# The norm of the SSD branch, the turned softmax statistics and the order of the first loads in a hybrid decoder layer

## The chip, the cores and the metric

The kernel runs on one core of one Trainium2 chip. The core has a matmul engine (PE, whose weight loads are listed apart as PEld), a vector engine (DVE), a scalar engine (ACT), a general engine (POOL), and the queue of SyncE (SP), which issues most of the DMAs; ACT issues a few. Each engine works through its own instructions in order and waits on semaphores for the others. The metric is the device time of one execution in microseconds (us), here as the median of three runs.

## What is computed

One layer of a decoder on x of shape (1, 512, 1024) in float32: norm, one projection of 1024 x 10,128, three branches side by side (dilated window attention, causal pooling, a Mamba-2 state-space branch, called SSD here), gates, an output projection, and a feed-forward block with a convolution. These are the parts that matter here:

```python
def rmsnorm(x, g):
    xf = x.astype(jnp.float32)
    y = xf * lax.rsqrt(jnp.mean(xf * xf, axis=-1, keepdims=True) + NORM_EPS)
    return (y * g.astype(jnp.float32)).astype(x.dtype)
...
    m = jnp.max(scores, axis=-1, keepdims=True)
    p = jnp.exp(scores - m)
    l = jnp.sum(p, axis=-1)
...
    lse = m[..., 0] + jnp.log(l)
...
    y = y.reshape(b, s, SSD_INNER) * jax.nn.silu(z.astype(jnp.float32))
    yg = y.reshape(b, s, SSD_GROUPS, SSD_INNER // SSD_GROUPS)
    yg = yg * lax.rsqrt(jnp.mean(yg * yg, axis=-1, keepdims=True) + NORM_EPS)
    y = yg.reshape(b, s, SSD_INNER) * norm_w.astype(jnp.float32)
```

The attention is done in three groups of six heads; each gives an output, a maximum and a sum per head and position, and the three groups are combined by a softmax over m + log(l). The SSD branch has two groups of 512 channels, each normed over its channels.

## The kernel before

**Number format.** A large product is made of three matmuls in the type fp32r (a rounded float32): each operand is split into a high part (a cast on ACT) and a low part (the difference, on DVE), and high x high, high x low and low x high are added in PSUM (`mm3`, L228). Small products are plain float32, and PE executes each of those as two passes, so that a count of matmuls in the trace is twice that in the code.

**Jobs and steps.** The large products are a list of jobs (`program`, L1430). A job loads its weights through SP into one of two buffers (`fetch`, L174), ACT casts the high part in two halves (`cast`, L186), DVE makes the low part (`low`, L219), and PE multiplies. At the start of job n the low part of job n+1, the casts of n+2 and the load of n+3 are written out. After each chunk of 128 output channels (24 matmuls of 128 x 512) the kernel calls `step` (L156), which advances every small task that is under way (attention items, SSD items, norms) by one `yield`. A `yield WHOLE` puts the part that follows behind the others' parts of the same step. The order of the instructions on PE, ACT, DVE and POOL is the order in which the code writes them out; only SP's order is left to the scheduler.

**Start.** x is loaded as four blocks of 128 rows in two halves each (`load_x`, L1498): block 0 by SP, block 1 by ACT, then ACT loads the identity matrix `eye` (L1506) and the gain of the first norm, and SP the first two weights and blocks 2 and 3. PE multiplies `ones` with itself twelve times meanwhile (L1515). The squares of a half row are summed on ACT or DVE (`squares`, L433); the factor of a block goes into a diagonal matrix (`diag`, L1586, made from `eye`), and PE turns and scales x in one matmul with it (L1574). For block 1 both halves are squared on ACT (L1579). `turned` (L1541, instructions L1544 and L1545) writes the high and low part of the result, and `begin` (L1548, matmuls L1557) starts the first two jobs on it. Blocks 2 and 3 are scaled on ACT and DVE (L1609, L1611) and turned by PE at L1622.

**Attention statistics.** In each group, `nm` holds the negated maxima and `ls` the sums, 128 positions x 4 blocks x 6 heads. `stats` (L781) turns each by four PE transposes into a PSUM tile `pst`, and DVE copies the 6 x 512 result (L788). After the third group, `combine` (L796) works out the weights: minima, differences, exponentials on ACT, sums, a reciprocal on DVE (L811), three products on POOL (L815), a store to DRAM (`wd`), and loads of it spread over partitions (`wb`, L822), two for each of nine tiles. POOL multiplies the nine attention outputs by them (L824), three for each pair of heads.

**Norm of the SSD branch.** z is multiplied onto y on DVE (L1088) and squared on ACT (L1090); the squares of a group's four tiles (128 channels x 512 positions each) are added by POOL, and the last one by DVE (L1094). `y_norm` (L1096) then does this for each group: four float32 matmuls with the tile of squares as the stationary operand and one column of ones (L1104) give the sums per position in a column form, `rstd_of` (L418) makes the factor of 4 columns with a square root on ACT and one Newton step on DVE, DVE spreads the factors into four diagonal blocks `dg` (L1108), three steps later a matmul of `ones` with `dg` (L1115) puts them into all rows of a PSUM tile `prb`, and DVE multiplies y by the norm weight and by `prb` (L1118). High and low parts follow (L1120, L1125), for `w_c`.

**Order around the norms.** `MIX` (L1674) is "ZZ0zz1ggggaa": two jobs for z of group 0, the norm of group 0 queued, two jobs for z of group 1, the norm of group 1 queued, four jobs of the third gate, two jobs of the attention branch; then the SSD branch's output product, which needs both norms. `combine` runs in the same steps.

Of the kernel before, what the change touches and what calls it, by code (L numbers as in the profile page):

```python
# [10 lines left out]
F32 = mybir.dt.float32  # L11
# [5 lines left out]
P = 128  # L17
S = 512
# [65 lines left out]
def trunk(ctx: ExitStack, tc, out, x, rel_bias, ln1_g, w_in, b_gate, w_a, pool_w, pool_scale, w_b,  # L84
# [23 lines left out]
    def T(name, dt=F32, shape=(P, S)):  # L108
        return big.tile(list(shape), dt, name=name, tag="t")
# [4 lines left out]
    def SM(name):  # L114
        return psum.tile([P, S], F32, name=name, tag="sm")
# [3 lines left out]

    eye = cpool.tile([P, P], F32, name="eye")  # L120
    tri = cpool.tile([P, P], F32, name="tri")
    ones = cpool.tile([P, P], F32, name="ones")


    waiting, running = [], []
# [440 lines left out]
    def blocked(ap, g):  # L566
        return ap.rearrange("p (r j) -> p r j", r=4) if g == 0 else perm(ap, g)
# [2 lines left out]
        return ap if g == 0 else ap.rearrange("p (r j) -> p r j", r=4)  # L570

    dtr = cpool.tile([P, 4, SH], F32, name="dtr")
    V, QK, OT, NM, LS = {}, {}, {}, {}, {}

    def v_jobs(g):
# [129 lines left out]
                                                          lambda i, ps: emit("q", 1, i, r3[i], ps))]  # L705

    def attend(g):
        nm = cpool.tile([P, 4, HEADS], F32, name=f"nm{g}")
        ls = cpool.tile([P, 4, HEADS], F32, name=f"ls{g}")
        if g == 0:  # L710
            banks = [[(1, 0, 2), (2, 1, 2)], [(3, 2, 2), (0, 0, 1)]]
        else:
# [67 lines left out]

        def stats():  # L781
            yield WHOLE
            for src, store, nme in ((nm, NM, "nmT"), (ls, LS, "lsT")):
                ps = SM("pst")
                for n in range(4):
                    pe.transpose(ps[:HEADS, n * P:(n + 1) * P], src[:, n, :], eye)
                t = T(nme)
                dve.tensor_copy(blocked(t[:HEADS], g), grouped(ps[:HEADS], g))  # L788
                store[g] = t

        fill([item(2 * c + hh, nb, bank) for c in range(3) for nb, bank in enumerate(banks)
              for hh in range(2)] + [after(2, stats())])
# [111 lines left out]
    def ssd_prep():  # L904
# [36 lines left out]
        yield WHOLE  # L941
        ps = SM("pcs")
        pe.matmul(ps[:, :n16], tri, a, start=True, stop=True)
        pe.matmul(ps[:, n16:2 * n16], ones, a, start=True, stop=True)
        for i, r in enumerate((dr, gr)):
            pe.transpose(ps[:, 2 * n16 + 8 * i:2 * n16 + 8 * i + 8], r[:8, :P], eye[:8, :8])
        dve.tensor_copy(dgc, ps[:, 2 * n16:2 * n16 + 16])
        acs, tot, dec = (f(nme) for nme in ("acs", "tot", "dec"))
        dve.tensor_copy(acs, ps[:, :n16])
        dve.tensor_copy(tot, ps[:, n16:2 * n16])  # L950
        dve.tensor_tensor(dec, tot, acs, OP.subtract)
# [31 lines left out]

    def ssd_item(c, gi):
        cs = slice(c * P, (c + 1) * P)
        dtv, acs, dec, tot, ad, ed = (cst[n] for n in ("dtv", "acs", "dec", "tot", "ad", "ed"))
        als = []
        for q in range(2):
            al = T("al")
# [106 lines left out]
    def y_norm(gi):  # L1096
        while len(SQ[gi]) < 4:
            yield
        yield
        yield  # L1100
        yield WHOLE
        ps = SM("pss")
        for tb in range(4):
            pe.matmul(ps[:, tb:tb + 1], SQ[gi][0][:, tb * P:(tb + 1) * P], ones[:, :1],  # L1104
                      start=True, stop=True)
        r = rstd_of(ps[:, :4], 4, S)
        dg = T("dg")
        dve.tensor_tensor(dg.rearrange("p (b t) -> p b t", b=4), eye.unsqueeze(1).to_broadcast([P, 4, P]),  # L1108
                          r.unsqueeze(2).to_broadcast([P, 4, P]), OP.mult)
        yield  # L1110
        yield
        yield
        yield WHOLE
        ps = SM("prb")
        pe.matmul(ps, ones, dg, start=True, stop=True)  # L1115
        for j in range(4):
            y, m = Y[gi][:, j, :], 4 * gi + j
            dve.scalar_tensor_tensor(y, y, cst["dgc"][:, 8 + m:9 + m], ps, OP.mult, OP.mult)  # L1118
            yh, yl = T("yth", F32R), T("ytl", F32R)
            act.copy(yh, y)  # L1120
            YT[m] = (yh, yl)
            if j % 2:
                yield
                for q in (m - 1, m):
                    dve.tensor_sub(YT[q][1], Y[gi][:, q % 4, :], YT[q][0].bitcast(F32))  # L1125
# [369 lines left out]

    xin, warm = {}, small("warm", [P, 1])

    def load_x(tb, eng=sp):  # L1498
        for h in range(2):
            t = xin[tb, h] = T("xin")  # L1500
            eng.dma_start(t, x[tb * P:(tb + 1) * P, h * S:(h + 1) * S])

    g8, g1 = T("g8"), cpool.tile([P, KD], F32, name="g1")
    load_x(0)
    load_x(1, act)
    act.dma_start(eye, c_eye)  # L1506
    act.dma_start(g8[:KD, :P], ln1_g[0].rearrange("(k p) -> k p", p=P))
    dve.memset(ones, 1.0)
    dve.memset(warm, 1.0)
    act.activation(warm, warm, AF.Sqrt)  # L1510
    first = [MM("pa") for _ in range(4)]

    def warm_up(n):
        for i in range(n):
            pe.matmul(first[3][:, :P], ones, ones, start=True, stop=True)  # L1515

    fetch(weights[0], 2)
    fetch(weights[1])
# [57 lines left out]
    for tb in range(2):  # L1576
        s0, s1, v, sq, r, rt = (small(n, [P, 1]) for n in ("s0", "s1", "v", "sq", "r", "rt"))
        squares(act, xin[tb, 0], s0)
        squares((dve, act)[tb], xin[tb, 1], s1)  # L1579
        dve.tensor_scalar(v, s0, 1.0 / D, EPS, OP.mult, OP.add)  # L1580
        dve.scalar_tensor_tensor(v, s1, 1.0 / D, v, OP.mult, OP.add)
        act.activation(sq, v, AF.Sqrt)
        dve.reciprocal(r, sq)
        dve.scalar_tensor_tensor(rt, r, v, r, OP.mult, OP.mult)
        dve.tensor_scalar(rt, rt, -0.5, 1.5, OP.mult, OP.add)
        dve.tensor_scalar(diag[tb][:, :P], eye, r, rt, OP.mult, OP.mult)  # L1586
        if tb == 0:
            for k in range(KD):
                turn_scale(0, k)
# [116 lines left out]
```

## Time and profile before

| | us |
|---|---|
| median of three runs (1039.3 to 1040.51) | 1039.63 |
| the profiled execution | 1039.95 |
| its span, from the first to the last instruction | 1038.0 |
| PE busy in 0 to 14 | 11.00 of 14 |
| PE busy in 505 to 570 (both norms, `combine`) | 65.00 of 65 |
| DVE busy in 505 to 570 | 47.95 of 65 |
| ACT busy in 505 to 570 | 34.43 of 65 |
| PE busy in 692 to 990 (feed-forward block) | 297.96 of 298 |
| PE busy in 990 to 1038 | 40.82 of 48 |

Busy times are those of instructions that an engine executes; a matmul overlaps the next one, so the distance between starts tells more of PE than the length of one. A line of the timeline has start, length, engine, line, operation, output <- inputs, shapes and count, and in brackets the idle time before it and what ended that. A line of the windows has the window, its length, busy time and count for PE, PEld, DVE, ACT and POOL, then the granted clock of PE as a share of full speed, the busy share of the DMA engines, and GB/s. The queue of SP is called q1 in the DMA views, that of ACT q10.

### The profile page before, as it was taken

What the parts mean: (1) busy time and instruction counts of PE and PEld (TensorE: products, weight loads), DVE (VectorE), ACT (ScalarE), POOL (GpSimd) and SP (SyncE); (2) the same over time, 40 slices, a digit from 0 to 9 for tenths busy, and PEclk for the clock granted to TensorE, in tenths of its full rate; (3) what the DMA queues carried; (4) which work ended last, traced back from release to release, by engine and by line L of the source; (5) the groups of instructions that cost most, each with busy time, mean ns of one, the idle gap of its engine ahead of it and who ended that gap; (6) DMA issues with size and microseconds to landing.
All of it is one profiled execution on the core that took longest, in us unless ns stands there. A gap on an engine that the chain in (4) does not pass through costs nothing.

```text
span 1038.0 us, 13344 instructions
## 1 busy us (share of the span) xinstructions
PE 1026.6 (99%) x5304; PEld 863.0 (83%) x5304; DVE 707.7 (68%) x947; ACT 488.7 (47%) x790; POOL 136.9 (13%) x118
## 2 busy tenths in 40 slices
PE   8999999999999999999999999999999999999997
PEld 8988877899888887788888888898888888888885
DVE  4563556778756649566658756767778769876776
ACT  5432445444574362566554324545445544444332
POOL 1680000000000001100143500001111100111002
PEclk9999999999999999999999999999999999999999
DMA  8445222124322354541253525443231232412222
GB/s 272 130 108 157 85 79 75 31 77 147 123 82 81 82 158 107 141 136 48 81 154 124 200 82 203 166 142 122 82 107 56 81 122 89 155 41 81 81 81 82
DMA packets 112302, 115.54 MB, mean 111 GB/s; under 512 B 5204, under 2 KB 97175, under 8 KB 112240
## 3 DMA queue, kind: packets, MB, share of 16 engines
q1 hardware_dynamic: 111647, 113.83, 35.5%
q8 instruction: 42, 0.69, 0.3%
q10 hardware_dynamic: 592, 0.86, 0.2%
q14 instruction: 21, 0.16, 0.1%
HBM read 110.87 MB, written 2.22 MB: 109 GB/s over the span
## 4 chain that ended last, share of the span: by engine, by line
PE 94%; DMA 2%; DVE 2%; ACT 1%; issue 1%; ACTq 0%; DVEq 0%; SPq 0%
PE pa L234 35%; PE pu L234 22%; PE pb L234 11%; PE pd L234 7%; PE pqk L234 6%; PE pa L1557 2%; PE pu L1363 1%; PE pq L234 1%; PE ps L731 1%; PE pt L760 1%; PE ppw L234 1%; PE po L772 1%; DMA w<-in_w_in_dram 1%; PE py L1045 1%; DMA eye<-in_c_eye_dram 1%
## 5 line engine op out<-in xcount | busy, mean ns | idle before, releaser
L215 DVE TENSOR_TENSOR wl<-raw,wh 128x2048 fp32r<-128x2048 f32 (+3 forms) x93 | 213.4, 2295 | 47.8 <-ACT wh L195 42.5
L195 ACT CAST wh<-raw 128x1024 fp32r<-128x1024 f32 (+3 forms) x184 | 183.6, 1017 | 40.1 <-DMA raw<-in_ffn_w_down_dram 12.9
L234 PE MATMUL pa<-uh,wh 128*128 128x512 f32 x384 | 99.5, 401 | 0.0
L1236 DVE SCALAR_TENSOR_TENSOR hc<-pu,fcol,hc 128x510 f32<-128x510 f32 x88 | 65.8, 748 | 49.0 <-ACT hc L1233 47.3
L234 PE MATMUL pa<-ul,wh 128*128 128x512 f32 x384 | 95.0, 389 | 0.0
L234 PE MATMUL pa<-uh,wl 128*128 128x512 f32 x384 | 94.8, 389 | 0.0
L234 PEld LDWEIGHTS pa<-ul,wh 128*128 128x128 f32 x384 | 72.1, 188 | 15.3
L234 PEld LDWEIGHTS pa<-uh,wl 128*128 128x128 f32 x384 | 72.1, 188 | 14.9
L234 PE MATMUL pu<-uh,wh 128*128 128x512 f32 (+1 forms) x352 | 83.6, 379 | 0.0
L234 PE MATMUL pu<-uh,wl 128*128 128x512 f32 (+1 forms) x352 | 83.5, 379 | 0.0
L234 PE MATMUL pu<-ul,wh 128*128 128x512 f32 (+1 forms) x352 | 83.5, 379 | 0.0
L234 PEld LDWEIGHTS pa<-uh,wh 128*128 128x128 f32 x384 | 70.2, 188 | 15.6 <-issue 1.7
L234 PEld LDWEIGHTS pu<-uh,wl 128*128 128x128 f32 x352 | 64.2, 188 | 12.4
L234 PEld LDWEIGHTS pu<-ul,wh 128*128 128x128 f32 x352 | 64.2, 188 | 12.4
L234 PEld LDWEIGHTS pu<-uh,wh 128*128 128x128 f32 x352 | 64.1, 188 | 12.4
L1241 POOL TENSOR_TENSOR hc<-hc 128x512 f32<-128x512 f32 x22 | 31.7, 1441 | 288.6 <-DVE hc L1236 253.6
L1233 ACT ACTIVATE hc<-pu,fcol,fcol 128x512 f32<-128x512 f32 x40 | 31.2, 780 | 79.1 <-PE pu L234 79.1
L1013 POOL TENSOR_TENSOR xd<-xc,dec 128x512 f32<-128x512 f32 x6 | 6.4, 1061 | 357.3 <-issue 308.8
L753 ACT ACTIVATE sb<-sb,nm 128x128 f32<-128x128 f32 (+1 forms) x72 | 30.1, 419 | 30.4 <-DVE nm L750 17.7
L1134 ACT ACTIVATE sg<-pa,col 128x512 f32<-128x512 f32 x24 | 16.5, 688 | 46.1 <-PE pa L234 46.1
L215 DVE TENSOR_TENSOR wl<-w,wh 128x2048 fp32r<-128x2048 f32 (+1 forms) x14 | 29.9, 2136 | 5.4 <-ACT wh L195 5.4
L1238 ACT ACTIVATE hc<-hc 128x512 f32<-128x512 f32 x22 | 13.9, 632 | 40.8 <-DVE hc L1236 40.8
(371 smaller groups left out, 1886.6 us busy)
## 6 DMA issues: line engine op xcount, KB each, us to landing
raw<-in_w_in_dram SPq DMA_DIRECT2D x25, 1024.0 KB, 6.3
raw<-in_ffn_w_up_dram SPq DMA_DIRECT2D x22, 1024.0 KB, 5.3
raw<-in_w_o_dram SPq DMA_DIRECT2D x8, 1024.0 KB, 5.1
raw<-in_w_in_dram SPq DMA_DIRECT2D x14, 512.0 KB, 4.1
raw<-in_ffn_w_down_dram SPq DMA_DIRECT2D x6, 1024.0 KB, 5.0
raw<-in_w_in_dram SPq DMA_DIRECT2D x6, 768.0 KB
raw<-in_w_b_dram SPq DMA_DIRECT2D x4, 1024.0 KB, 5.0
al<-ad SPq DMA_DIRECT2D x16, 256.0 KB, 7.0
```

The costliest lines, as they stand in the source:

```text
L195: act.copy(job.high[:, :, o], job.raw[:, :, o])
L215: (eng or dve).tensor_tensor(l[:, :, o], job.raw[:, :, o], h[:, :, o].bitcast(F32), OP.subtract)
L234: pe.matmul(ps, l, r, start=first and n == 0, stop=last and n == total - 1)
L731: pe.matmul(pss[i][:, o:o + w * P], q[r, n * P:(n + 1) * P], k[r, kb * P:(kb + w) * P], start=True, stop=True)
L753: act.activation(sb[:, off:off + w * P], sb[:, off:off + w * P], AF.Exp, bias=nm[:, n, h:h + 1], accum_out=ls[:, n, h:h + 1])
L760: pe.transpose(pt[:, o:o + P], sb[:, o:o + P], eye)
L1134: act.activation(s, ps, AF.Sigmoid, bias=col[:, o:o + 1])
L1233: act.activation(t, ps, AF.Identity, bias=ff["c1"][:, ff["b"] + m:ff["b"] + m + 1], scale=fw(2, m))
L1236: dve.scalar_tensor_tensor(t[:, sh:], ps[:, :S - sh], fw(k, m), t[:, sh:], OP.mult, OP.add)
L1238: act.activation(t, t, AF.Silu)
L1241: pool.tensor_tensor(a, a, t, OP.mult)
L1557: pe.matmul(first[2 * n + j][:, lo:hi], a[:, k, j * P:(j + 1) * P], b[:, k, lo:hi], start=a is wh and b is uh and k == 0, stop=a is wl and ...
```

## The change

`ones` becomes an fp32r tile (its float32 uses are reinterpreted). The norm of a group splits the summed squares into a high part on ACT and a low part on DVE and multiplies each by the 128 x 128 matrix of ones, so that each row of PSUM holds the sums of all positions; the factor is worked out on whole 128 x 512 rows: logarithm, exponential with -1/2 and square on ACT, and one Newton step in two DVE operations, up to a constant (-0.5/512) that goes into the norm's weight column once. The diagonal blocks and the second matmul are gone. The statistics of a group share one tile, `nm` in columns 0 to 5 and `ls` in columns 32 to 37 with zeros between, which is turned by four transposes; the tile serves all three groups. Two of the SSD's constant tiles take the buffers of earlier intermediate values. The halves of blocks 0 and 1 of x are loaded by SP and ACT side by side, `eye` ahead of the second half of block 1, and the square of that half moves from ACT to DVE. In the built program all orders on PE, ACT, DVE and POOL outside these parts are the same; on SP one load of a weight (the last of the third gate) comes before the first four `wb` loads and no longer after them. The weight low part (L215) that stood behind the factor's DVE work in the first norm is ahead of it now, since that work is written out a step later, and in the second norm the low part of the squares stands behind the first two products (L1118, in the changed kernel L1123) of the first norm.

```diff
--- before.py
+++ after.py
@@ -119,7 +119,8 @@
 
     eye = cpool.tile([P, P], F32, name="eye")
     tri = cpool.tile([P, P], F32, name="tri")
-    ones = cpool.tile([P, P], F32, name="ones")
+    ones = cpool.tile([P, P], F32R, name="ones")
+    eps = cpool.tile([P, 1], F32, name="eps")
 
 
     waiting, running = [], []
@@ -570,6 +571,8 @@
         return ap if g == 0 else ap.rearrange("p (r j) -> p r j", r=4)
 
     dtr = cpool.tile([P, 4, SH], F32, name="dtr")
+
+    both = cpool.tile([P, 4, 32 + HEADS], F32, name="nmls")
     V, QK, OT, NM, LS = {}, {}, {}, {}, {}
 
     def v_jobs(g):
@@ -705,8 +708,7 @@
                                                           lambda i, ps: emit("q", 1, i, r3[i], ps))]
 
     def attend(g):
-        nm = cpool.tile([P, 4, HEADS], F32, name=f"nm{g}")
-        ls = cpool.tile([P, 4, HEADS], F32, name=f"ls{g}")
+        nm, ls = both[:, :, :HEADS], both[:, :, 32:]
         if g == 0:
             banks = [[(1, 0, 2), (2, 1, 2)], [(3, 2, 2), (0, 0, 1)]]
         else:
@@ -780,13 +782,12 @@
 
         def stats():
             yield WHOLE
-            for src, store, nme in ((nm, NM, "nmT"), (ls, LS, "lsT")):
-                ps = SM("pst")
-                for n in range(4):
-                    pe.transpose(ps[:HEADS, n * P:(n + 1) * P], src[:, n, :], eye)
-                t = T(nme)
-                dve.tensor_copy(blocked(t[:HEADS], g), grouped(ps[:HEADS], g))
-                store[g] = t
+            ps = SM("pst")
+            for n in range(4):
+                pe.transpose(ps[:32 + HEADS, n * P:(n + 1) * P], both[:, n, :], eye)
+            for at, store, nme in ((0, NM, "nmT"), (32, LS, "lsT")):
+                t = store[g] = T(nme)
+                dve.tensor_copy(blocked(t[:HEADS], g), grouped(ps[at:at + HEADS], g))
 
         fill([item(2 * c + hh, nb, bank) for c in range(3) for nb, bank in enumerate(banks)
               for hh in range(2)] + [after(2, stats())])
@@ -941,11 +942,12 @@
         yield WHOLE
         ps = SM("pcs")
         pe.matmul(ps[:, :n16], tri, a, start=True, stop=True)
-        pe.matmul(ps[:, n16:2 * n16], ones, a, start=True, stop=True)
+        pe.matmul(ps[:, n16:2 * n16], ones.bitcast(F32), a, start=True, stop=True)
         for i, r in enumerate((dr, gr)):
             pe.transpose(ps[:, 2 * n16 + 8 * i:2 * n16 + 8 * i + 8], r[:8, :P], eye[:8, :8])
-        dve.tensor_copy(dgc, ps[:, 2 * n16:2 * n16 + 16])
-        acs, tot, dec = (f(nme) for nme in ("acs", "tot", "dec"))
+        dve.tensor_copy(dgc[:, :8], ps[:, 2 * n16:2 * n16 + 8])
+        dve.tensor_scalar(dgc[:, 8:], ps[:, 2 * n16 + 8:2 * n16 + 16], -0.5 / S, None, OP.mult)
+        acs, tot, dec = (f(nme) for nme in ("acs", "dts", "dtz"))
         dve.tensor_copy(acs, ps[:, :n16])
         dve.tensor_copy(tot, ps[:, n16:2 * n16])
         dve.tensor_tensor(dec, tot, acs, OP.subtract)
@@ -983,7 +985,7 @@
 
     def ssd_item(c, gi):
         cs = slice(c * P, (c + 1) * P)
-        dtv, acs, dec, tot, ad, ed = (cst[n] for n in ("dtv", "acs", "dec", "tot", "ad", "ed"))
+        dtv, acs, dec, tot, ad, ed = (cst[n] for n in ("dtv", "acs", "dtz", "dts", "ad", "ed"))
         als = []
         for q in range(2):
             al = T("al")
@@ -1096,26 +1098,29 @@
     def y_norm(gi):
         while len(SQ[gi]) < 4:
             yield
-        yield
+        qh, ql = T("sqh", F32R), T("sql", F32R)
+        act.copy(qh, SQ[gi][0])
+        yield
+        dve.tensor_sub(ql, SQ[gi][0], qh.bitcast(F32))
         yield
         yield WHOLE
+
         ps = SM("pss")
-        for tb in range(4):
-            pe.matmul(ps[:, tb:tb + 1], SQ[gi][0][:, tb * P:(tb + 1) * P], ones[:, :1],
-                      start=True, stop=True)
-        r = rstd_of(ps[:, :4], 4, S)
-        dg = T("dg")
-        dve.tensor_tensor(dg.rearrange("p (b t) -> p b t", b=4), eye.unsqueeze(1).to_broadcast([P, 4, P]),
-                          r.unsqueeze(2).to_broadcast([P, 4, P]), OP.mult)
-        yield
-        yield
-        yield
-        yield WHOLE
-        ps = SM("prb")
-        pe.matmul(ps, ones, dg, start=True, stop=True)
+        pe.matmul(ps, ones, qh, start=True, stop=False)
+        pe.matmul(ps, ones, ql, start=False, stop=True)
+        r, t = T("yr"), T("yt")
+        act.activation(r, ps, AF.Ln, bias=eps, scale=1.0 / S)
+        act.activation(r, r, AF.Exp, scale=-0.5)
+        act.activation(t, r, AF.Square)
+        yield
+
+        dve.scalar_tensor_tensor(t, ps, S * EPS, t, OP.add, OP.mult)
+        dve.scalar_tensor_tensor(r, t, -3.0 * S, r, OP.add, OP.mult)
+        yield
+        yield
         for j in range(4):
             y, m = Y[gi][:, j, :], 4 * gi + j
-            dve.scalar_tensor_tensor(y, y, cst["dgc"][:, 8 + m:9 + m], ps, OP.mult, OP.mult)
+            dve.scalar_tensor_tensor(y, y, cst["dgc"][:, 8 + m:9 + m], r, OP.mult, OP.mult)
             yh, yl = T("yth", F32R), T("ytl", F32R)
             act.copy(yh, y)
             YT[m] = (yh, yl)
@@ -1495,24 +1500,26 @@
 
     xin, warm = {}, small("warm", [P, 1])
 
-    def load_x(tb, eng=sp):
+    def load_x(tb, engs=(sp, sp)):
         for h in range(2):
             t = xin[tb, h] = T("xin")
-            eng.dma_start(t, x[tb * P:(tb + 1) * P, h * S:(h + 1) * S])
+            engs[h].dma_start(t, x[tb * P:(tb + 1) * P, h * S:(h + 1) * S])
 
     g8, g1 = T("g8"), cpool.tile([P, KD], F32, name="g1")
-    load_x(0)
-    load_x(1, act)
+    load_x(0, (sp, act))
     act.dma_start(eye, c_eye)
+    load_x(1, (sp, act))
     act.dma_start(g8[:KD, :P], ln1_g[0].rearrange("(k p) -> k p", p=P))
-    dve.memset(ones, 1.0)
+    dve.memset(ones.bitcast(F32), 1.0)
+    dve.memset(eps, EPS)
+    dve.memset(both, 0.0)
     dve.memset(warm, 1.0)
     act.activation(warm, warm, AF.Sqrt)
     first = [MM("pa") for _ in range(4)]
 
     def warm_up(n):
         for i in range(n):
-            pe.matmul(first[3][:, :P], ones, ones, start=True, stop=True)
+            pe.matmul(first[3][:, :P], ones.bitcast(F32), ones.bitcast(F32), start=True, stop=True)
 
     fetch(weights[0], 2)
     fetch(weights[1])
@@ -1576,7 +1583,7 @@
     for tb in range(2):
         s0, s1, v, sq, r, rt = (small(n, [P, 1]) for n in ("s0", "s1", "v", "sq", "r", "rt"))
         squares(act, xin[tb, 0], s0)
-        squares((dve, act)[tb], xin[tb, 1], s1)
+        squares(dve, xin[tb, 1], s1)
         dve.tensor_scalar(v, s0, 1.0 / D, EPS, OP.mult, OP.add)
         dve.scalar_tensor_tensor(v, s1, 1.0 / D, v, OP.mult, OP.add)
         act.activation(sq, v, AF.Sqrt)
```

## Prediction

> **What bounds the kernel now.** First the page's busy times:
>
> ```profile
> span 1038.0 us, 13344 instructions
> PE 1026.6 (99%) x5304; PEld 863.0 (83%) x5304; DVE 707.7 (68%) x947; ACT 488.7 (47%) x790; POOL 136.9 (13%) x118
> ```
>
> PE is idle for 11.4 us in all, so time comes only from PE work that goes away, from PE idling, or from a lower PE clock. The chain of waits of the first 40 us shows where a good part of the idling is:
>
> ```profile
> 1.66 6.33 DMA eye<-in_c_eye_dram
> ...
> 8.09 0.35 DVE diag L1586
> ...
> 8.51 2.50 PE uT L1574 x16
> 11.00 0.20 PE pa L1590
> 11.20 3.01 PE uT L1574 x16
> 14.21 9.59 PE pa L1557 x80
> ```
>
> PE stands from 6.54 (end of the warm-up) to 8.49, and the second sixteen passes take 3.0 us where the first take 2.5. The windows of one us give the reason (the number before the DMA share is the granted clock):
>
> ```profile
> 9.00:10.00 1.00, 1.00 (x11) 1.00 (x11) 0.87 (x4) 0.97 (x2) 0.00 (x0) 0.95 1.11 323
> 10.00:11.00 1.00, 1.00 (x6) 0.78 (x5) 0.02 (x1) 1.00 (x1) 0.99 (x1) 0.50 1.09 348
> ```
>
> The trace's clock record has half clock from 9.90 to 13.32, one stretch of 3.41 us, after a stretch of 3.41 us (6.49 to 9.90) in which PE was busy for 43%.
>
> Then the changed PE instructions, in the timeline of PE, with the first main-loop matmuls after each:
>
> ```profile
> 508.48 0.60 PE L786 MATMUL pst<-eye,nm 128*6 128x128 f32 x4
> 508.92 0.60 PE L786 MATMUL pst<-eye,ls 128*6 128x128 f32 x4
> 509.27 2.07 PE L234 MATMUL pa<-uh,wh 128*128 128x512 f32 x8
> ...
> 525.69 0.94 PE L1104 MATMUL pss<-ones,sq 128*128 128x1 f32 x8
> ...
> 542.97 1.02 PE L1115 MATMUL prb<-dg,ones 128*128 128x512 f32 x2
> ```
>
> Last DVE and POOL around the second norm, in their timelines:
>
> ```profile
> 544.21 1.76 DVE L1094 TENSOR_TENSOR sq<-sq 128x512 f32<-128x512 f32 x1 [7.59 <-POOL sq L1094]
> 545.90 3.37 DVE L215 TENSOR_TENSOR wl<-raw,wh 128x2048 fp32r<-128x2048 f32 x1
> 549.20 1.39 DVE L1118 SCALAR_TENSOR_TENSOR xs<-xs,dgc,prb 128x512 f32<-128x512 f32 x2
> ...
> 541.66 1.29 POOL L824 TENSOR_TENSOR o<-o,wb 128x512 f32<-128x512 f32 x1 [3.90 <-DMA wb<-wd]
> 542.91 1.27 POOL L1094 TENSOR_TENSOR sq<-sq 128x512 f32<-128x512 f32 x1
> 544.13 7.54 POOL L824 TENSOR_TENSOR o<-o,wb 128x512 f32<-128x512 f32 x4
> ```
>
> The same DVE operations cost 0.67 (L1094 at 510.94) and 2.29 us (L215 at 532.64) alone. The two engines take turns: 1.76 is one POOL multiply of some 1.1 left plus 0.67.
>
> **Part 1, the loads (gain 1.75).** x[0]'s right half (x01) goes to the head of ACT's queue, where x[1]'s left half was. That queue (q10) had moved 0.24 MB by 4.0, so its first 0.26 MB land near 4.7; x01's square on DVE now starts at 5.78 on a DMA wait: 1.05 sooner (bounds 0 and 1.25, ACT's start on x00 at 4.53). eye is next in the queue, so the 0.47 that DVE waits for it before L1586 goes too: first diag at 6.55, PE at 6.95. The square of x11, moved to DVE, adds 0.69 behind it; from the next v (7.5) to the end of the second diag is 1.67 (8.35 to 10.02), so 9.2. ACT's first square root of tb 1 comes at 7.9, then its two casts of weight 0 (2.1). Their loads keep their places behind the same bytes, and the second cast began at 9.95 with no wait, so its load lands by then: casts end between 10.2 and 11.0; I take 10.8. The eight L1544 (0.42 each) then end at 14.25 instead of 16.19, since PE's passes are there in time even at half clock. What hangs on ACT (squares of x[2] and x[3], L1611) moves with it and sets L1622, at 23.64 before with 0.2 to spare. I take 1.75; bounds 0.9 (casts at 11.0, late x11) and 2.2.
>
> **Part 2, statistics (gain 1.05).** Eight transposes become four, three times. The second four take 0.36, 0.36 and 0.35 to the next start (0.045 a pass); the first four 0.44, with the switch in it. The stationary operand grows from 6 to 38 columns: 64 columns (L772, 16 passes in 1.03) go at 0.064. So 0.28 to 0.44 each; I take 0.35.
>
> **Part 3, the norm's matmuls (gain 2.61).** Pitch returns to the steady 0.227 (72 in 16.34) only with the second L234 after them, at 526.82 and 544.06; counted back one pitch, pss holds PE for 0.90 and prb for 0.86. Two fp32r products cost 2 x 0.227 = 0.45. Saved: 1.76 - 0.45 = 1.31, twice. If the products cost an fp32 pass each (0.43), 0.9.
>
> **Part 4, a new wait (loss 4.3).** Before, pss(1) at 549.28 needed only the sum of squares from DVE (done 545.97). Now it needs sql, and in the built order DVE does: sum L1094, weight low part L215, two products of group 0, then sql. Times below are those of before, with PE's saving of 1.31 on norm 0 taken off: PE wants sql at 549.28 - 1.31 + 0.23 = 548.2. The chain: sql of group 0 (0.6) goes ahead of the reciprocal at 522.80, so POOL's L815 and the wd stores come 0.7 later; SP's order has the next weight load ahead of all wb loads, no longer between the fourth and fifth. It is issued at 531.3 (before 534.98); 4.7 later its bytes are in (as before: wb landed at 541.66, two wb loads and their lag after it). wb pairs then land at 537.5, 538.3, 539.0, and POOL runs three multiplies of 1.25 and the sum to 542.55 (before 544.2: sooner by 1.6). From there DVE and POOL alternate: multiply to 543.8, DVE sum 544.45, multiply 545.7, L215 547.95, multiply 549.2, product 549.85, multiply 551.1, product 551.8, sql 552.45. PE waits 4.3.
>
> The products' price decides here. L1118 read one operand from PSUM and cost 738 ns beside POOL; now both tensors are in SBUF. The nearest row with that is L858:
>
> ```profile
> 47.01 0.68 DVE L858 SCALAR_TENSOR_TENSOR pd<-psw,pu 128x512 f32<-128x512 f32 x1
> 49.49 1.50 DVE L858 SCALAR_TENSOR_TENSOR pd<-psw,pu 128x512 f32<-128x512 f32 x1 [0.36 <-POOL psw L852]
> ```
>
> so I take it as blocked. By L1118's price the products take 1.4 from 547.95, sql one turn more: 551.1 at worst, 550.0 free: waits of 1.8 to 2.9. [...] Bounds of the wait: 2.0 (wb 1 us sooner, last multiply out of the way) and 6.5 (below).
>
> **Part 5, the clock (loss 1.6).** A wait of 4.3 in a row of 3.41-us stretches leaves one of them at most 37% busy, below the 43% that cost the clock at 9.90. One stretch at half clock has 512-column products at 0.43 for 0.227: 3.41 x (1 - 0.227/0.43) = 1.6. Bounds 0 and 2.3 (two stretches touched). [...]
>
> **At nothing:** two memsets and a split dgc copy (0.1 to 0.2 each, the memsets before ACT's table load ends at 4.17, the copy on a DVE that is 68% busy); per norm one more table load (1.28), qh, Ln, Exp and Square (0.6 to 0.7 each) on ACT, which idles 2.85 before the sigmoid at 532.33 and whose result is read a step later; the PSUM bank of pa freed 1.7 later is one of four, each used once in 21.8. Uncovered they would be some 4 us a norm. The shared nmls tile adds no wait in the built order; each group's turn is read long before the next group writes.
>
> **Sum:** -1.75 - 1.05 - 2.61 + 4.3 + 1.6 = +0.5. The profiled execution took 1039.95 (span 1038.0 and 1.95 around it), 0.3 over the median of 1039.63; on the median: **1040.1**, no change.
>
> **Rivals.** [...] (b) The wait is short (1.8, products as L1118) and the clock stays: 1039.63 - 5.41 + 1.8 = 1036.0; with no wait at all 1034.2. L858 speaks against, POOL's idling before 542 for. (c) Slower: the weight load ahead of the wb loads makes POOL's third multiply no sooner than before, 542.3 with the late reciprocal, not 540.0: sql at 554.7, wait 6.5, two stretches of half clock 2.3: 1039.63 - 5.41 + 8.8 = 1043.0. It decides once wait plus clock pass 7.5. For it: today's third multiply waits 3.90 on such a load; against: that load was issued 3.7 later. (d) The loads bring nothing, because x01 shares the engines as before: +1.75, 1041.9; against: q10 and q1 moved equal bytes from 2 to 4.
>
> **Numbers.** Forecast 0.45, (a) 0.15, (b) 0.20, (c) 0.14, (d) 0.06. Range 1036.0 to 1042.8; the forecast's own 1038.3 to 1041.8. About 0.2% (2.1 us) is what a measurement of this kernel can tell from no change. Faster: (b) and a part of (a) and of the forecast's low tail, 0.27. Slower: (c), (d) in part, and the upper tail, 0.23. Same: 0.50.
>
> **What would show it.** The first L1574 near 7.0 and L1622 near 21.8 (part 1); pst for 0.5 (part 2); pss as two products in 0.45 and no prb (part 3); PE idle before the second product of the second pss, released by DVE's sql, some 4 us, with the products before it at 1.1 or more each (part 4); a stretch of half clock near it (part 5). Wrong if that idle is under 2 us or the clock stays at 1.00.

## The result, and the profile after

The changed kernel takes 1042.1 us (median of 13 runs, 1041.1 to 1043.1) against 1039.45 us for the kernel before in the same session (13 runs, 1037.6 to 1040.5). The ratio is 1.0025, 95% interval 1.0017 to 1.0032: slower by 2.6 us. The time on record was 1040.1 with a range of 1036.0 to 1042.8; the result lies in it, at its upper end, but 0.3 above the forecast's own range (1038.3 to 1041.8) and just above the 2.1 us that were called no change.

The profiled execution of after took 1041.17, its span is 1039.1. The page's busy times:

```profile
span 1039.1 us, 13285 instructions
PE 1022.8 (98%) x5276; PEld 860.0 (83%) x5276; DVE 711.3 (68%) x944; ACT 494.7 (48%) x796; POOL 139.8 (13%) x118
```

PE has 3.8 us less work than before (1026.6) and the span is 1.1 longer, so PE idles 4.9 us more. The waits of PE (engine and what waited, what it waited for, us in total, times, longest) have one new entry, and it is the largest:

```profile
PE pss L1110 <- DVE sql L1104: 6.1, 1, 6.1
PE pa L1522 <- DVE ones L1513: 1.1, 1, 1.1
PE uT L1581 <- DVE diag L1593: 0.9, 2, 0.5
```

The start, in the chain of waits of the first 40 us (start, us, what):

```profile
1.66 5.83 DMA xin<-in_x_dram
...
9.78 2.05 PE uT L1581 x16
11.83 9.67 PE pa L1564 x80
21.50 1.75 PE uT L1629 x16
```

In the timeline of PE the two groups of sixteen transposes take 2.15 and 2.05 now; before they took 2.52 and 3.08. The first matmuls behind them (L1564) start at 11.83 instead of 14.21.

The statistics and both norms in the timeline of PE (start, us, engine, line, operation, count, idle before and its releaser):

```profile
504.63 0.62 PE L787 MATMUL pst<-eye,nmls 128*38 128x128 f32 x4
505.01 1.18 PE L235 MATMUL pa<-uh,wh 128*128 128x512 f32 x4
...
521.45 0.39 PE L1109 MATMUL pss<-sqh,ones 128*128 128x512 f32 x1
521.68 0.39 PE L1110 MATMUL pss<-sql,ones 128*128 128x512 f32 x1
521.91 2.01 PE L235 MATMUL pa<-uh,wh 128*128 128x512 f32 x8
...
543.94 0.50 PE L1109 MATMUL pss<-sqh,ones 128*128 128x512 f32 x1
550.53 0.80 PE L1110 MATMUL pss<-sql,ones 128*128 128x512 f32 x1 [6.10 <-DVE sql L1104]
551.12 3.06 PE L235 MATMUL pa<-uh,wh 128*128 128x512 f32 x8
```

Up to 505.01 PE is 4.26 us ahead of before (509.27). The first norm costs two products and nothing else. At the second, PE stands for 6.10 us, and the eight products behind it take 3.06 where eight take 1.98 elsewhere: the window of 545 to 560 has a granted clock of 0.77. What PE waits for is seen in the timelines of DVE and POOL:

```profile
541.47 1.76 DVE L1096 TENSOR_TENSOR sq<-sq 128x512 f32<-128x512 f32 x1 [10.27 <-POOL sq L1096]
543.15 3.38 DVE L216 TENSOR_TENSOR wl<-raw,wh 128x2048 fp32r<-128x2048 f32 x1
546.45 3.42 DVE L1123 SCALAR_TENSOR_TENSOR xs<-xs,dgc,yr 128x512 f32<-128x512 f32 x2
549.80 0.68 DVE L1104 TENSOR_TENSOR sql<-sq,sqh 128x512 fp32r<-128x512 f32 x1
...
522.63 6.16 POOL L816 TENSOR_TENSOR nmT<-nmT,dtmp 6x512 f32<-6x512 f32 x3 [19.84 <-DVE dtmp L812]
528.76 1.28 POOL L1096 TENSOR_TENSOR sq<-sq 128x512 f32<-128x512 f32 x1
536.41 3.79 POOL L825 TENSOR_TENSOR o<-o,wb 128x512 f32<-128x512 f32 x3 [6.36 <-DMA wb<-wd]
540.15 1.29 POOL L1096 TENSOR_TENSOR sq<-sq 128x512 f32<-128x512 f32 x1
541.39 7.93 POOL L825 TENSOR_TENSOR o<-o,wb 128x512 f32<-128x512 f32 x4
```

DVE idles for 10.27 us until POOL's second addition of the squares of group 1 (540.15), which stands behind three multiplies by wb. Then the last addition, a weight's low part and two products of group 0 go ahead of sql, each stretched by POOL's multiplies: 1.76, 3.38 and 3.42 beside them, where the same takes 0.67 (507.29), 2.29 (512.33) and 1.41 (568.39) with POOL idle.

### The profile page after: what moved, and what is told of

Same layout as the page of the kernel before. It is cut to its first block, busy times and chain, and to the rows that moved or that the text cites. A ratio compares the mean times of both kernels' runs of the same rounds, so it can differ in the third digit from the quotient of the medians.

```text
span 1039.1 us, 13285 instructions
## 1 busy us (share of the span) xinstructions
PE 1022.8 (98%) x5276; PEld 860.0 (83%) x5276; DVE 711.3 (68%) x944; ACT 494.7 (48%) x796; POOL 139.8 (13%) x118
## 4 chain that ended last, share of the span: by engine, by line
PE 91%; DVE 3%; DMA 2%; ACT 1%; issue 1%; POOL 1%; SPq 0%; ACTq 0%; DVEq 0%; POOLq 0%
PE pa L235 31%; PE pu L235 22%; PE pb L235 12%; PE pd L235 7%; PE pqk L235 6%; PE pa L1564 2%; PE pq L235 2%; PE pu L1368 1%; PE ps L733 1%; PE pt L762 1%; PE ppw L235 1%; PE po L774 1%; DVE wl L216 1%; DMA wb<-wd 1%; DMA al<-ad 1%
## 5 line engine op out<-in xcount | busy, mean ns | idle before, releaser
L1015 POOL TENSOR_TENSOR xd<-xc,dtz 128x512 f32<-128x512 f32 x6 | 6.4, 1062 | 355.9 <-issue 307.4
L755 ACT ACTIVATE sb<-sb,nmls 128x128 f32<-128x128 f32 (+1 forms) x72 | 30.1, 419 | 30.4 <-DVE nmls L752 17.7
```

The lines of the kernel that those rows point to most:

```text
L755: act.activation(sb[:, off:off + w * P], sb[:, off:off + w * P], AF.Exp, bias=nm[:, n, h:h + 1], accum_out=ls[:, n, h:h + 1])
```

## The experiments

Every time below is a median, beside the same session's runs of before (1039.3 to 1039.5 in all four).

**norm_undone: the norm as before, loads and statistics changed.**

```
-        pe.matmul(ps, ones, qh, start=True, stop=False)
-        pe.matmul(ps, ones, ql, start=False, stop=True)
+        for tb in range(4):
+            pe.matmul(ps[:, tb:tb + 1], SQ[gi][0][:, tb * P:(tb + 1) * P], ones.bitcast(F32)[:, :1],
+                      start=True, stop=True)
...
+        pe.matmul(ps, ones.bitcast(F32), dg, start=True, stop=True)
```

> After with the norm as before the change (sums turned, factor spread by prb); the loads and the turned statistics stay changed. Theory (the norm alone costs time, by the wait of PE for sql): in the traces PE of after is 4.26 us ahead of before at 505, where the last pst lies, and nothing behind that is changed any more, so 1039.4 - 4.3 = 1035.2 (1034.6 to 1036.0). Rival (what loads and statistics win is given back later, since a DMA or DVE sets a later end): 1037 or more.

1036.13 us, ratio 0.9971 (0.9959 to 0.9982), 0.1 above the theory's range and well below the rival's 1037. The window of 545 to 560 has PE busy for all 15.00 and the clock at 1.00. So the two small parts win 3.3 us, and the norm on top of them loses 6.0.

**norm_alone: the changed norm on the kernel before.** The loads and the transposes of the statistics stay those of before; of the diff remain the parts of the norm:

```
-        yield WHOLE
-        ps = SM("prb")
-        pe.matmul(ps, ones, dg, start=True, stop=True)
...
+        pe.matmul(ps, ones, qh, start=True, stop=False)
+        pe.matmul(ps, ones, ql, start=False, stop=True)
```

> Before with the changed norm alone. Theory: PE of after goes from 4.26 us ahead of before at 505 to 1.1 behind at the end, so the norm costs 5.4 and the time is 1044.9 (1043.5 to 1046); PE waits some 6 us for sql of group 1 and shows half clock beside it. Rival (the wait comes from group 1 being reached sooner, by loads and statistics): the wait is about 2 and the time 1039 to 1041.

1042.98 us, ratio 1.0041 (1.0028 to 1.0054): +3.5, less than expected, but the wait is there, 5.4 us long, without loads or statistics, so the rival is ruled out. The trace also shows a reason for the time below the expectation. It has the old loads, and yet its start lost no clock (timeline of PE; L1580 are the transposes of the two first token blocks):

```profile
8.16 2.05 PE L1580 MATMUL uT<-diag,xin 128*128 128x128 f32 x16 [1.70 <-DVE v L1586]
10.15 0.22 PE L1596 MATMUL pa<-eye,g 8*128 8x8 f32 x1
10.30 2.05 PE L1580 MATMUL uT<-diag,xin 128*128 128x128 f32 x16
12.11 0.72 PE L1563 MATMUL pa<-uh,wh 128*128 128x256 f32 x4
```

PE waits 1.70 here, 1.95 in the profile of before; there the clock fell for 3.41 us (0.98 over the window of 0 to 100), here it did not (1.00 over the same window), and the first pst comes at 190.05 instead of 191.91.

**loads_alone and stats_alone: one part each on the kernel before.**

```
-    load_x(0)
-    load_x(1, act)
+    load_x(0, (sp, act))
     act.dma_start(eye, c_eye)
+    load_x(1, (sp, act))
...
-        squares((dve, act)[tb], xin[tb, 1], s1)
+        squares(dve, xin[tb, 1], s1)
```

```
-            for src, store, nme in ((nm, NM, "nmT"), (ls, LS, "lsT")):
-                ps = SM("pst")
-                for n in range(4):
-                    pe.transpose(ps[:HEADS, n * P:(n + 1) * P], src[:, n, :], eye)
+            ps = SM("pst")
+            for n in range(4):
+                pe.transpose(ps[:32 + HEADS, n * P:(n + 1) * P], both[:, n, :], eye)
```

> Before with the halved x loads (and the square of x[1]'s right half on DVE) alone. Theory: the start of the profile before lost a stretch of clock that the same start doesn't always lose (norm_alone, with the old loads, reached its first pst at 190.0; before at 191.9, after at 189.6), so the loads are worth 0.4 where the clock stays and 2.3 where it falls; over many runs 1037.3 to 1038.9. Rival (they always bring the 2.3 that the two traces show): 1036.8 to 1037.2.

> Before with both statistics turned at once, alone (two short-lived names share a buffer, as in after). Theory: four passes for eight, three times at 0.35 to 0.5: 1039.4 - 1.05 to 1.5 = 1037.9 to 1038.4. Rival (PE's gain is given back at the sums, which wait for POOL and DVE): 1039.4.

loads_alone: 1037.89, ratio 0.9989 (0.9980 to 0.9997), 1.6 us faster, as the theory had it. Its 11 runs all have a mean granted clock of 0.998 or 0.999. Of the 68 runs of the kernel before in the first three sessions, 51 have spans of 1036.9 us or more (median 1037.5) and 17 shorter ones (median 1035.7, all but one of these with a clock of 0.998 or 0.999). Of the 51 longer ones 40 have a mean clock of 0.997 or less. So, by the mean clock, the old start loses its stretch in most executions, the new one in none seen; and against the short runs of before (1035.7) the loads' own runs (median span 1035.8) are no faster. So most of what this part brings is clock. stats_alone: 1037.40, ratio 0.9979 (0.9970 to 0.9989), 2.1 us faster, somewhat more than the theory. Its trace gives 0.37 for each turn and norm_alone's gives 0.79 to 0.80, so 1.26 for the three comes from the passes; 6 of its 11 runs have spans of 1035.4 to 1037.0, the others 1033.9 to 1034.4, so the long kind was rarer here than in before (51 of 68), which may account for the rest.

The three medians of the parts alone (-1.6, -2.1, +3.5) add up to -0.2, where after has +2.6. The traces show that the norm itself is not what differs: from the last pst to branch a PE takes 63.61 in before and in norm_undone, 68.79 in norm_alone and 68.99 in after, so it costs 5.2 to 5.4 with or without the other parts. What differs lies ahead of it, where norm_alone's trace is 2.5 ahead of before's at the last pst; 1.9 of this are there at the first pst already, behind the start that kept its clock. These are single executions, so how much of the gap between the medians this makes up is not shown.

**pe_busy: PE kept busy while it waits.** The 24 products go into a bank that nobody reads.

```
         pe.matmul(ps, ones, qh, start=True, stop=False)
+        if gi:
+            idle = SM("idle")
+            for _ in range(24):
+                pe.matmul(idle, ones, qh, start=True, stop=True)
```

> After with 24 products of sqh into a bank that nobody reads, between the two products of the second pss, so that PE is busy while it waits. Theory (6.8 us at half clock beside the wait cost 1.4 us): the wait ends at the same time (near 550.5), the clock stays at 1.00 in 545 to 560, the next L235 are at 0.227 at once, and the time is 1042.1 - 1.4 - 0.4 = 1040.3 (1039.9 to 1040.8). Rival (the low clock costs nothing, or is not due to the idling): 1041.5 to 1042.5.

1040.29, ratio 1.0010 (1.0001 to 1.0019), 1.8 less than after. The second product came at 551.03, no sooner than in after, and the clock of 545 to 560 is 1.00:

```profile
544.71 5.78 PE L1113 MATMUL idle<-sqh,ones 128*128 128x512 f32 x24
551.03 0.50 PE L1114 MATMUL pss<-sql,ones 128*128 128x512 f32 x1 [0.54 <-DVE sql L1104]
551.36 1.99 PE L235 MATMUL pa<-uh,wh 128*128 128x512 f32 x8
```

The theory holds: the clock lost beside the wait is a cost of its own, and it is due to PE's idling (PE busy for 14.46 of the 15.00 in 545 to 560 with a clock of 1.00, for 9.47 with 0.77 in after; mean clock 0.998 or 0.999 in its 11 runs, 0.994 or 0.995 in the 13 of after). From the second product to branch a PE takes 22.10, where it takes 23.47 in after.

**r_psum: the factor in PSUM.**

```
-        dve.scalar_tensor_tensor(r, t, -3.0 * S, r, OP.add, OP.mult)
+        dve.scalar_tensor_tensor(ps, t, -3.0 * S, r, OP.add, OP.mult)
...
-            dve.scalar_tensor_tensor(y, y, cst["dgc"][:, 8 + m:9 + m], r, OP.mult, OP.mult)
+            dve.scalar_tensor_tensor(y, y, cst["dgc"][:, 8 + m:9 + m], ps, OP.mult, OP.mult)
```

> After with the factor written over the sums in PSUM, so that the four products of each group read one operand from PSUM as before the change. Theory (two SBUF operands make them wait for POOL): the two products ahead of sql take 1.4 for 3.4 us, sql is 1.7 to 2 sooner, PE waits 4.1 to 4.4 and loses one stretch of clock less: 1039.4 to 1040.2. Rival (they are late by the queue on DVE and by POOL's turn, not by their operand): the wait stays at 5.5 or more and the time at 1041 to 1042.5.

1040.36, ratio 1.0014 (1.0005 to 1.0022). DVE's timeline:

```profile
546.41 1.39 DVE L1123 SCALAR_TENSOR_TENSOR xs<-xs,dgc,pss 128x512 f32<-128x512 f32 x2
547.72 1.66 DVE L1104 TENSOR_TENSOR sql<-sq,sqh 128x512 fp32r<-128x512 f32 x1
```

The two products fell from 3.42 to 1.39, as expected. But sql, which also reads two tensors from SBUF, now met a multiply of POOL and took 1.66 instead of 0.68, so half of the gain was handed on: the wait is 4.95, not 4.1 to 4.4, and the time is 0.2 above the theory's range. Half clock lasts one stretch of 3.41 instead of two (0.89 in 545 to 560, 0.77 in after).

**sql_early: sql written in the step of sqh.**

```
         act.copy(qh, SQ[gi][0])
-        yield
         dve.tensor_sub(ql, SQ[gi][0], qh.bitcast(F32))
         yield
+        yield
         yield WHOLE
```

> After with the low part sql written right behind sqh, in the same step, so that on DVE it stands ahead of the weight's low part and the two products of group 0. Theory (the wait is the queue on DVE): sqh ends at 543.9, sql between 544.6 and 545.9, PE wants it at 544.1: a wait of 0.5 to 1.8 for 6.1 and a clock that stays full; 1042.1 - 4.3 to 5.6 - 1.4 = 1035.1 to 1036.4. Rival (the weight's low part, now 1 to 2 us later, makes PE wait in its place): the wait moves to an L235 row and the time is 1037 to 1040.

1040.50, ratio 1.0013 (1.0004 to 1.0022). Neither case: the queue on DVE was shortened for group 1, but the same edit made DVE wait for ACT in group 0:

```profile
511.66 0.67 DVE L1090 TENSOR_TENSOR xs<-xs,zs 128x512 f32<-128x512 f32 x1
516.92 0.69 DVE L1103 TENSOR_TENSOR sql<-sq,sqh 128x512 fp32r<-128x512 f32 x1 [4.58 <-ACT sqh L1102]
...
523.67 3.33 DVE L812 RECIPROCAL dtmp<-den 6x512 f32<-6x512 f32 x1
```

Everything queued behind that instruction on DVE, the attention denominators and their reciprocal among it, came some 4 us later, and with it wd, wb, POOL's additions and so the sum of group 1 itself. PE then waited 3.57 for sqh and 0.23 for sql.

**pss_later: the second norm's products one chunk later.**

```
         yield
+        if gi:
+            yield
         yield WHOLE
```

> After with the second norm's two products one step (one chunk of 128 channels, 5.45 us on PE) later. Theory: sql is ready at about 550.5, PE reaches the second product at 549.6, so the wait is 0 to 0.9, the clock stays full, and the time is 1042.1 - 6.1 - 1.4 + 0 to 0.9 = 1034.6 to 1035.5. Rival (what reads the factor is late in its turn, or the PSUM bank of pss): PE waits elsewhere and the time stays above 1037.

1040.65, ratio 1.0016 (1.0008 to 1.0025). The wait for sql is 0.83, as the theory had it, and the rival came true: 3.48 and 0.66 are lost at the first products of branch a, and one stretch of half clock follows (from 572.25; 0.91 over the window of 560 to 575). PE's and ACT's timelines:

```profile
566.82 0.61 PE L235 MATMUL pa<-ah,wh 128*128 128x512 f32 x2
570.91 0.50 PE L235 MATMUL pa<-ah,wh 128*128 128x512 f32 x1 [3.48 <-ACT ah L833]
571.25 0.62 PE L235 MATMUL pa<-al,wh 128*128 128x512 f32 x2
572.53 0.80 PE L235 MATMUL pa<-al,wh 128*128 128x512 f32 x1 [0.66 <-DVE al L836]
```

```profile
561.46 0.62 ACT L833 CAST ah<-o 128x512 fp32r<-128x512 f32 x1 [4.57 <-DVE o L831]
562.10 1.28 ACT L1114 ACT_TABLE_LOAD   x1
563.39 0.69 ACT L1114 ACTIVATE yr<-pss,eps 128x512 f32<-128x512 f32 x1
564.10 1.28 ACT L1115 ACT_TABLE_LOAD   x1
...
570.24 0.62 ACT L833 CAST ah<-o 128x512 fp32r<-128x512 f32 x1 [0.77 <-DVE o L831]
```

The norm's Ln, Exp and Square with three table loads (562.10 to 568.05) now stand ahead of the third ah on ACT, and DVE's part of the norm waits for them ahead of the o sum that ah needs. In after, the stalled PE reached branch a at 574.00, when all of it was done (third ah at 566.84): its first wait hid a second one.

**factor_dve: the three products of nmT off POOL.**

```
-            pool.tensor_tensor(n, n, tmp[:HEADS], OP.mult)
+            dve.tensor_tensor(n, n, tmp[:HEADS], OP.mult)
```

> After with the three products of nmT with the reciprocal on DVE, ahead of the weight's low part, instead of on POOL beside it (6.2 us there, 4.0 before the change). Theory (they make wd, and with it wb and POOL's sum of squares, late): wd goes out by 525, the weight load at 527.1 when the low part has freed its buffer, wb 2.1 sooner, the sum 2 sooner, the wait of PE for sql 4.1 for 6.1, one stretch of half clock less: 1042.1 - 2 - 0.7 = 1039.4 (1038.7 to 1040.2). Rival (wb is bound by the weight load's bytes alone): the wait stays within 0.5 of 6.1 and the time at 1041.5 to 1042.5.

1041.83, ratio 1.0027 (1.0017 to 1.0036), and the wait is 6.1: the rival. The queue of SP and POOL's timeline:

```profile
523.33 1.46 SPq L817 DMA_DIRECT2D wd<-nmT  x3
527.34 0.39 SPq L184 DMA_DIRECT2D raw<-in_w_in_dram  x1
527.83 12.48 SPq L823 DMA_DIRECT2D wb<-wd  x14
...
536.70 3.78 POOL L825 TENSOR_TENSOR o<-o,wb 128x512 f32<-128x512 f32 x3 [15.34 <-DMA wb<-wd]
```

wd goes out 4 us sooner than in after (where its three issues end at 529.07), the weight load and wb 1.9 sooner, and POOL's first multiply starts 0.3 later (536.41 in after). The weight load took 8.7 us to land where it takes 6.1 in after.

**own_queue: that weight load on ACT's queue, out of SP's.**

```
+    own = weights[52]
...
-                        fetch(weights[n + 3])
+                        fetch(weights[n + 3], eng=act if weights[n + 3] is own else sp)
```

> After with the weight load that stands between the wd stores and the wb loads in SP's queue given to ACT's queue, where it follows norm 0's Square (at 528.4, no wait there in after). Theory (wb, and through it POOL's sum and sql, is late because its packets come behind that load's 1 MB): the first o multiply on POOL starts at 533.5 to 535 for 536.4, the sum of squares and sql come as much sooner, PE waits 3.2 to 4.7 for 6.1, with one stretch of half clock for two at best; 1038 to 1040.7. Rival (the 16 engines share the bytes, whatever the queue): the first multiply at 536 or later, the wait at 5.7 or more, 1041.5 to 1042.6.

1042.79 over 5 runs (1041.2 to 1044.4), ratio 1.0041 (1.0027 to 1.0054): no gain, and above the rival's range too. In its trace POOL's first multiply starts at 535.08, 1.3 sooner, and the wait is 4.9, 1.2 shorter; between the two cases. ACT also issues the load 1.2 sooner than SP did (527.96 for 529.18), as much as the multiply gains, so this run does not part the queue from the earlier issue. The time did not follow, since the half clock lay otherwise: by the clock record from 548.17 to 555.00 (0.77 over 545 to 560; in windows of one us 1.00 from 547 to 548, 0.50 from 554 to 555, 1.00 from 555 to 556), with PE at work in all but the first microsecond of it, where in after it lay from 546.54 to 553.37, more than half of it under the wait. From the second product to branch a PE takes 24.84 here (549.21 to 574.05), 23.47 in after (550.53 to 574.00) and 22.03 in sum_dve below, where the clock is full: 2.8 lost here, 1.4 in after.

**sum_dve: the additions of squares of group 1 all on DVE.**

```
-            (dve if len(SQ[gi]) == 4 else pool).tensor_tensor(SQ[gi][0], SQ[gi][0], sq, OP.add)
+            (dve if len(SQ[gi]) == 4 or gi else pool).tensor_tensor(SQ[gi][0], SQ[gi][0], sq, OP.add)
```

> After with the additions of squares of group 1 all on DVE (two of them were POOL's, and stood behind its o multiplies). Theory (what makes everything late is that the sum of squares waits in POOL's queue until 541.4, while DVE idles for 10.3 us before it): the sum is ready near 532 to 534, sql near 538 at the latest, PE doesn't wait at the second product (wants it at 544.1), the clock stays, the norm's Ln, Exp and Square run on ACT by 550 and are out of the way of ah; 1042.1 - 6.1 - 1.4 = 1034.6 (1033.8 to 1035.8). Rival (POOL's multiplies of o are late by themselves, wd and the weight load ahead of wb being so): PE then waits for ah of the third pair at the first L235 of branch a, and the time stays above 1037.

1034.24 (5 runs, 1033.0 to 1036.0), ratio 0.9956 (0.9943 to 0.9968): 5.1 us faster than before and 7.9 faster than after. DVE and PE:

```profile
533.69 0.69 DVE L1096 TENSOR_TENSOR sq<-sq 128x512 f32<-128x512 f32 x1 [0.84 <-ACT sq L1092]
...
540.82 1.78 DVE L1104 TENSOR_TENSOR sql<-sq,sqh 128x512 fp32r<-128x512 f32 x1
...
543.77 0.39 PE L1109 MATMUL pss<-sqh,ones 128*128 128x512 f32 x1
544.00 0.39 PE L1110 MATMUL pss<-sql,ones 128*128 128x512 f32 x1
544.23 2.01 PE L235 MATMUL pa<-uh,wh 128*128 128x512 f32 x8
```

The sum is complete at 534.4, in time that DVE idled before; sql comes at 542.6, not by 538, but still 1.4 ahead of PE; the wait is gone, and the clock of 545 to 560 is 1.00. Branch a starts at 566.03 with no wait: with POOL rid of two additions and the norm's ACT work done by 558.3, the third ah (563.29) is in time too.

**undone_sum: the same edit on norm_undone.**

> norm_undone (loads and statistics changed, the norm as before) with the additions of squares of group 1 all on DVE, as in sum_dve. Theory (without the changed norm nothing waits for that sum, so moving it brings nothing, and all that sum_dve gains on norm_undone is the two products for sums and prb): 1036.1 (1035.6 to 1036.6). Rival (POOL's relief is a gain by itself): 1034.2 to 1035.2.

1035.92, ratio 0.9969 (0.9956 to 0.9981), as norm_undone. So the edit brings nothing where no one waits for the sum. Between the last pst and branch a, PE takes 60.96 in sum_dve (505.07 to 566.03) and 63.61 in norm_undone (505.19 to 568.80): the norm's matmuls are worth 2.65.

## Why the prediction was near, and which step was off

The mechanism was right: PE idle before the second product of the second pss, released by DVE's sql, with products of 1.7 each ahead of it, and half clock beside it. What failed is the size of the wait in part 4, 4.3 predicted and 6.10 measured, and what came true there is rival (c), held at 0.14. That the time still lies in the range is in part luck: that rival's own price, 1043.0, stood just outside it, and the clock took 1.4 of the 2.3 that it allowed.

| term | predicted | measured |
|---|---|---|
| part 1, loads | -1.75 | -2.3 between the two traces, -1.6 in loads_alone |
| part 2, statistics | -1.05 | -1.26 from the passes, -2.1 in stats_alone |
| part 3, norm's matmuls | -2.61 | -2.65 |
| part 4, wait for sql | +4.3 | +6.10 idle; 6.6 with the first product 0.24 late and run to its end (0.50) where the next one else starts after 0.23 |
| part 5, clock | +1.6 | +1.4 in after's trace, 2.8 in own_queue's |

**Part 4.** From the sum to sql the prediction had 9.9 us (542.55 to 552.45) and the trace has 9.0 (541.44 to 550.48): the order on DVE, and the price of a product with two SBUF operands beside POOL (3.42 for two, 1.39 with one in PSUM in r_psum), were read rightly from L858. The step that failed is "It is issued at 531.3 (before 534.98); 4.7 later its bytes are in", and what was hung on it, POOL's addition done at 542.55. In after's time that is 538.3 (4.26 sooner); it was done at 541.44, 3.1 late. The weight load was issued at 529.18, not 527.0, because wd left late: the weight's low part (3.18 at 523.21) now ran beside POOL's three products, which took 6.16 for 4.04 before; the prediction had moved them 0.7 later, but priced them as before, when DVE was busy for 1.34 of the 4.04 beside them.

```profile
526.28 4.04 POOL L815 TENSOR_TENSOR nmT<-nmT,dtmp 6x512 f32<-6x512 f32 x3 [19.64 <-DVE dtmp L811]
```

```profile
523.21 3.18 DVE L216 TENSOR_TENSOR wl<-raw,wh 128x2048 fp32r<-128x2048 f32 x1 [0.18 <-ACT wh L196]
...
529.18 0.48 SPq L184 DMA_DIRECT2D raw<-in_w_in_dram  x1
```

The first line is before's, the other two (DVE, and the queue of SP) are after's. The load then took 6.1 to land, with wb behind it: from its issue to the first multiply 7.2, where the prediction had 6.2. factor_dve took the first cause away and the second grew (9.4 from the issue to the multiply); so the delay is not that of the products alone. Rival (c), that the weight load ahead of wb makes POOL's third multiply no sooner than before, priced at a wait of 6.5 and 1043.0, is what happened: in the time of before (4.26 later) the third multiply starts at 543.2 (538.90 in after), where it started at 541.66, and sql is done at 554.7, to the tenth what (c) had. Not all of it is for (c)'s reason: 2.1 of the 3.1 are POOL's slower products, which neither the forecast nor a rival had. Rival (d), 1041.9, is nearer to the time by number alone, but its condition failed: loads_alone is 1.6 faster than before.

**Part 5.** One stretch was predicted, two came, at about the predicted cost in after's trace. own_queue shows that the same two stretches can cost twice as much when they begin later against the wait (2.8 for 1.4). Whether that makes up the spread of after's runs (spans of 1039.0 to 1041.0) was not tried; the profiled one is among the shortest, and its span is only 1.1 above before's where the medians differ by 2.6.

**Part 1.** The transposes began at 7.01 (7.0 predicted) and L1629 at 21.50 (21.8). The chain was right to some half a microsecond (the second diagonal ends at 9.74, 9.2 predicted), but the worth was read as work that starts sooner; most of it is a stretch of clock that, by the mean clock, the old start loses in most executions (0.997 or less in 41 of 68 runs of before), and the new one did not lose (0.998 or 0.999 in all 11 of loads_alone). The prediction saw that stretch in before, but had the new start bear "half clock" as well and gave its return no term of its own.

**Part 3** came out to 0.04, and pss took 0.46 and prb is gone, as predicted; pst took 0.38 for the 0.5 that was named. **At nothing** holds in after, where PE has no wait from those instructions; pss_later shows the price of the norm's ACT work once the cover is gone, 4.1 us of waiting for ah and al.

The 6.6 of part 4 is what PE loses from the last pst to the second product against sum_dve (45.52 for 38.93). By the traces, -4.26 to the last pst, of which 0.7 lies between the changed places, then -2.65 + 6.6 + 1.4: together +1.1, as the spans differ. Of the 0.7, 0.5 lies between the first pst and the second (136.66 in before): loads_alone, whose code is the same there, takes 136.16. So that part comes with before's profiled execution and not from the change; why it is slower there is open.

## What to carry to other kernels

When a reduction is cut over to one step that needs a second, derived operand, ask when the last input of that operand is ready, and which engine adds it up: here an addition on the wrong queue was worth nearly 8 us, and moving it into another engine's idle time turned a loss of 2.6 into a gain of 5.1. A wait of the engine that sets the pace hides the ones behind it, so removing it (pss_later, 6.10 us down to 0.83) is worth only the distance to the next late operand (4.14 more behind it). And an instruction moved ahead on an in-order engine takes its own wait along, to everything behind it (sql_early, 4.58 us on DVE).

## What the runs showed of the hardware

Half clock lasted 3.413 us at before's start (9.91 to 13.32) and 6.827 us, twice that, beside after's wait (546.54 to 553.37). In these runs what followed a stretch of 3.41 us went with how busy PE was in it; pe_busy, which changed little else, kept the clock at 1.00 in 545 to 560, where after has 0.77. At full clock, stretches with PE busy for about 0% (own_queue), 16% (sql_early), 28% (pss_later), 36% (after) and 43% (before's start) were followed by half clock, and those with about 50% (norm_alone's start, a wait of 1.70) and 55% (r_psum) were not. At half clock, stretches busy for 0% (after), 30% (factor_dve), 70% (own_queue) and 73% (sql_early) were followed by another at half, and those with 83% (after) and 100% (r_psum) by full clock. The shares are worked out from the timelines and the record, some points wide, and PE's ends are modelled; the runs show these points and no more.

The two stretches at half clock lie differently against the same wait in after (546.54 to 553.37, the wait to 550.53) and own_queue (548.17 to 555.00, the wait to 549.21). The stretches busy for 36% and 43% were not idle, and cost the clock all the same.

In r_psum DVE's price for two SBUF operands moved along its queue: freed at one instruction (L1123, 3.42 to 1.39 for two), the next of the kind paid (sql, 0.68 to 1.66), since it now started at 547.72, while POOL's multiplies ran on (four in 541.34 to 548.84); in after it started at 549.80, behind the last of them (549.32).
